# An encoder trunk's instruction order: the scheduler's other simulator

## The chip, the cores and the metric

The kernel runs on one core of one Trainium2 chip. The metric is device time in microseconds (us) of one execution of the whole program, as the median of several runs. One execution was also recorded by the hardware profiler; every row of a profile below comes from such a recorded execution.

## The reference

Two layers of an encoder over 512 positions of width 1024, in float32. Each layer normalises its input, projects it once, feeds three attention mixers that run side by side (A: grouped queries with normalised heads and a two-axis rotation; B: the difference of two softmaxes; C: latent attention with low-rank queries and keys), gates and merges them, projects and adds; then an MLP with a squared ReLU. A last normalisation follows.

```python
for l in range(DEPTH):                      # 2
    h = _rms_norm(x, ln1_g[l])
    proj = jnp.einsum('bsd,dn->bsn', h, w_in[l])
    (a_q, a_k, a_v, b_q, b_k, b_v, c_cq, c_ckv, c_kr, gate_logits) = _split_columns(proj)
    y_a = _gqa_axial(...)                   # 8 heads of 64 on 2 key heads
    y_b = _diff_attention(...)              # 8 heads, 2 x 32 for q and k, 64 for v
    y_c = _mla(...)                         # 8 heads, 64 + 32 for q and k, 64 for v
    y = jnp.stack([y_a, y_b, y_c], axis=2)
    gates = jax.nn.sigmoid(gate_logits.reshape(b, s, N_BRANCH, d))
    merged = jnp.sum(gates * jnp.einsum('bsne,ned->bsnd', y, w_branch[l]), axis=2)
    x = x + jnp.einsum('bsd,de->bse', merged, w_out[l])
    h2 = _rms_norm(x, ln2_g[l])
    ff = jnp.square(jax.nn.relu(jnp.einsum('bsd,df->bsf', h2, w_ff1[l])))
    x = x + jnp.einsum('bsf,fd->bsd', ff, w_ff2[l])
return _rms_norm(x, final_g)
```

## The kernel before

**Arithmetic.** Every float32 operand of a large product is split into a high part in TensorE's rounded float32 type and the rest (h and l in the names: wh, wl, fh, fl), and a product is three matmuls: high by high, high by rest, rest by high. A weight arrives by a DMA from SP's queue into a raw buffer wr (L53), ACT casts it to wh (L61), and GpSimd or VectorE subtracts to get wl (L67): GpSimd in pieces of 256 columns, VectorE in one piece. There are two raw buffers (NWR) and three of each part (NW). In the mixers all weights are split on GpSimd (PA = 5), in the MLP all on VectorE (PF = 0). The MLP's second product uses a scheme with seven block products in place of eight; its factors fa and fs come by DMA, some of them added on arrival by accumulating DMAs that GpSimd issues (L95, L96), and are split at L115 and L116.

**Stages.** The plan of a layer is a list of small items, each with a cost in us that serves only to arrange the list. First the projections of A and half of those of B (tm, L309 and L322). Then attention A, with the rest of B's projections woven in; attention B, with gates, branch products (gate, br, in L222) and C's low-rank products (c_rank); attention C, with the remaining gates, branches and C's per-head products (uq, uk). After that the last branches, the output projection (out, L222) and the MLP in three chunks, each a first product (ff, L222) and a second (ff, L1152).

**An attention unit.** One head and 128 queries: scores sc on TensorE (L222), the row maximum mx on VectorE (L585), the exponential p with its sum on ACT (L590), scaling by the reciprocal on VectorE (L595, for B L747), four transposes pT on TensorE (L601), the cast and the rest pt on ACT and VectorE (L604, L605), and for each pair of units the product with the values, pv (L222). Transposes of the projections (tp, L338) and the rotations (a_t, c_t, b_r) stand between. The pv, pT, tp and sc results lie in eight PSUM banks by tag: two for scores, two for transposes, one for values and statistics, three for projections and other long products.

**What sets the order.** The Python program issues its instructions in the order of the plan, with some steps deferred by a time of the plan (`defer`, for example transposes by LAG_T = 5.5 after their scores). That is not yet the order on the chip. At the end of the `TileContext` block a scheduler simulates the program and picks for each engine, whenever the simulated engine can take one, the earliest instruction of the program that is ready by then. The order so found is written into each engine's queue, SP's and GpSimd's DMA issues included, and the buffer that a tile gets among those of its tag is decided on the way. On the chip each queue then runs strictly in that order: an instruction whose operand is late holds up all behind it on its engine.

```python
    with tile.TileContext(nc) as tc:
        Trunk(tc, a, depth).go()
```

Of the kernel before, what the change touches and what calls it, by code (L numbers as in the profile page):

```python
# [1360 lines left out]
def build(nc, arrays, depth):  # L1361
    a = {k: nc.dram_tensor(k, v.shape, F32, kind="ExternalInput").ap() for k, v in arrays.items()}
    a["out"] = nc.dram_tensor("out", (128, 8, S), F32, kind="ExternalOutput").ap()
    with tile.TileContext(nc) as tc:
        Trunk(tc, a, depth).go()


# [8 lines left out]
```

## Time and profile before

| what | us |
|---|---|
| median of 3 runs | 1872.87 |
| lowest and highest | 1872.87, 1876.54 |
| the profiled execution's own time | 1872.25 |
| its span, first to last instruction | 1870.4 |
| TensorE busy in the span | 1820.2 |
| mean granted TensorE clock | 0.993 |

The span is what the profile's rows count from; their times are us from its start. A row of the stage table gives a stretch and, for each engine, busy time and number of instructions. A row of the waits gives who stood idle, for what, how long in total, how often, and the longest. In a timeline row the bracket at the end says how long the engine had been idle before it and what released it. PE is TensorE, PEld its weight loads, DVE VectorE, ACT ScalarE, POOL GpSimd, and SPq the queue in which SP issues DMAs. "br<-ya,wh" names the tile written and those read.

### The profile page before, as it was taken

The page shows a single profiled execution, that of the slowest core. Times are in us where ns is not written, and L with a number is a line of the kernel's source. Part 1 is how long each engine was busy: PE and PEld are TensorE (multiplying, and loading weights), DVE is VectorE, ACT ScalarE, POOL GpSimd, SP SyncE. Part 2 cuts the span into 40 slices and gives each one's busy share as a digit, 9 for nine tenths or more (in the row PEclk, how much of TensorE's full clock was granted, in tenths as well). Part 3 has the DMA queues.
Part 4 walks back from the last instruction along what each step waited for, and adds up shares of the span by engine and source line. Part 5 has one row for each costly group of instructions (what it writes and reads, how often), then busy time and mean ns, then how long its engine had stood idle before and what let it go on. Part 6 is the DMA issues. An engine that isn't in the chain of part 4 may idle for free.

```text
span 1870.4 us, 29990 instructions
## 1 busy us (share of the span) xinstructions
PE 1820.2 (97%) x10960; PEld 1603.4 (86%) x10960; DVE 1386.2 (74%) x2815; ACT 1011.1 (54%) x1852; POOL 461.6 (25%) x565
## 2 busy tenths in 40 slices
PE   8999999999999999999999999999999999999997
PEld 8998888777888898988999988878888888989897
DVE  8888889755665776867887888896566667777677
ACT  5577666655544434444446766665554444444443
POOL 4322443444101100101243224434440001011011
PEclk9999999999999999999999999999999999999998
DMA  5213331332153473745532134312232525637363
GB/s 164 79 41 85 102 108 43 96 84 81 51 170 101 100 188 92 172 121 147 138 105 68 40 91 124 92 46 84 82 91 68 163 90 125 163 94 187 100 147 94
DMA packets 85058, 197.25 MB, mean 105 GB/s; under 512 B 11952, under 2 KB 28720, under 8 KB 84912
## 3 DMA queue, kind: packets, MB, share of 16 engines
q1 hardware_dynamic: 74544, 178.56, 31.8%
q0 software_dynamic: 10368, 16.78, 6.0%
q8 instruction: 87, 1.43, 0.3%
q14 instruction: 59, 0.48, 0.1%
HBM read 174.32 MB, written 4.19 MB: 95 GB/s over the span
## 4 chain that ended last, share of the span: by engine, by line
PE 76%; DVE 12%; ACT 4%; DMA 4%; issue 2%; POOL 1%; SPq 0%; DVEq 0%; ACTq 0%; POOLq 0%
PE ff L222 18%; PE ff L1152 15%; PE gate L222 12%; PE br L222 6%; PE tm L309 5%; PE out L222 4%; PE sc L222 4%; PE pv L222 4%; PE pT L601 4%; PE c_rank L222 2%; DMA wr<-w 2%; DVE mx L585 1%; DMA fa<-wff 1%; DVE wl L67 1%; DVE p L747 1%
## 5 line engine op out<-in xcount | busy, mean ns | idle before, releaser
L67 POOL TENSOR_TENSOR wl<-wr,wh 128x256 fp32r<-128x256 f32 (+1 forms) x402 | 298.2, 772 | 534.9 <-ACT wh L61 503.1
L61 ACT CAST wh<-wr 128x1024 fp32r<-128x1024 f32 (+5 forms) x246 | 224.6, 914 | 343.2 <-PE ff L222 114.0
L1152 PE MATMUL ff<-h,fh 128*128 128x256 f32 x1792 | 324.1, 283 | 1.4 <-DVE x L1160 1.2
L222 PE MATMUL ff<-xg,wh 128*128 128x512 f32 x1024 | 315.6, 390 | 0.0
L1152 PEld LDWEIGHTS ff<-h,fh 128*128 128x128 f32 x1792 | 278.9, 192 | 3.1 <-issue 2.1
L1152 PE MATMUL ff<-h,fl 128*128 128x256 f32 x896 | 254.2, 285 | 1.5 <-DVE fl L116 1.3
L222 PE MATMUL gate<-xg,wh 128*128 128x512 f32 x768 | 241.5, 393 | 1.1 <-DVE c_K L230 1.1
L222 PEld LDWEIGHTS ff<-xg,wh 128*128 128x128 f32 x1024 | 191.7, 188 | 39.3
L115 ACT CAST fh<-fa 128x640 fp32r<-128x640 f32 (+1 forms) x144 | 108.8, 762 | 177.5 <-PE ff L1152 94.2
L309 PE MATMUL tm<-wh,xg 128*128 128x256 f32 x1024 | 202.4, 289 | 0.0
L585 DVE TENSOR_REDUCE mx<-sc 128x1 f32<-128x512 f32 x256 | 173.7, 683 | 36.7 <-PE sc L222 35.7
L222 PE MATMUL ff<-xg,wl 128*128 128x512 f32 x512 | 199.2, 389 | 0.0
L1152 PEld LDWEIGHTS ff<-h,fl 128*128 128x128 f32 x896 | 171.0, 192 | 4.7 <-DVE fl L116 4.1
L222 PEld LDWEIGHTS gate<-xg,wh 128*128 128x128 f32 x768 | 142.8, 188 | 29.9 <-PE pv L222 1.5
L309 PEld LDWEIGHTS tm<-wh,xg 128*128 128x128 f32 x1024 | 164.7, 192 | 0.2
L67 DVE TENSOR_TENSOR wl<-wr,wh 128x1024 fp32r<-128x1024 f32 (+3 forms) x117 | 134.0, 1145 | 25.2 <-ACT wh L61 25.2
L116 DVE TENSOR_TENSOR fl<-fa,fh 128x640 fp32r<-128x640 f32 (+1 forms) x144 | 124.6, 869 | 36.9 <-ACT fh L115 33.6
L222 PE MATMUL gate<-xg,wl 128*128 128x512 f32 x384 | 150.5, 392 | 0.0
L604 ACT CAST pt<-pT 128x512 fp32r<-128x512 f32 x192 | 112.0, 585 | 64.3 <-PE pT L601 62.1
L605 DVE TENSOR_TENSOR pt<-pT,pt 128x512 fp32r<-128x512 f32 x192 | 131.2, 685 | 19.3 <-ACT pt L604 17.7
L309 PE MATMUL tm<-wl,xg 128*128 128x256 f32 x512 | 145.0, 283 | 0.0
L601 PE MATMUL pT<-ident,p 128*128 128x128 f32 x768 | 116.2, 274 | 10.5 <-DVE p L595 4.8
(253 smaller groups left out, 3515.6 us busy)
## 6 DMA issues: line engine op xcount, KB each, us to landing
wr<-w SPq DMA_DIRECT2D x170, 512.0 KB, 3.6
fa<-wff SPq DMA_DIRECT2D x64, 320.0 KB, 3.4
wr<-w SPq DMA_DIRECT2D x52, 256.0 KB, 2.8
fa<-wff SPq DMA_DIRECT2D x32, 384.0 KB, 3.8
b_sq<-b_f SPq DMA_DIRECT2D x96, 64.0 KB, 2.8
b_sk<-b_f SPq DMA_DIRECT2D x96, 64.0 KB, 2.0
fa<-wff POOLq DMA_DIRECT2D x16, 320.0 KB, 4.8
fs<-wff SPq DMA_DIRECT2D x32, 160.0 KB, 2.8
```

Source lines behind the costliest of these rows:

```text
L61: t.nc.scalar.copy(wh, self.raw)
L67: e.tensor_tensor(wl[:, q], self.raw[:, q], wh[:, q].bitcast(F32), op=ALU.subtract)
L115: t.nc.scalar.copy(a, x)
L116: t.nc.vector.tensor_tensor(b, x, a.bitcast(F32), op=ALU.subtract)
L222: self.nc.tensor.matmul(out, l, r, start=(i == 0), stop=(i == n - 1))
L309: self.nc.tensor.matmul(ps, l, r, start=(u == 0 and i == 0 and tt % 2 == 0), stop=(u == 1 and tt % 2 == 1 and i == len(p) - 1))
L585: nc.vector.tensor_reduce(m, s, axis=AX.X, op=ALU.max, negate=True)
L601: nc.tensor.transpose(T[:, k], p[:, k * 128 : (k + 1) * 128], self.ident)
L604: nc.scalar.copy(h[:, :, q], T)
L605: nc.vector.tensor_tensor(lo[:, :, q], T, h[:, :, q].bitcast(F32), op=ALU.subtract)
L747: nc.vector.scalar_tensor_tensor(p0, p1, z1, p0, op0=ALU.mult, op1=ALU.add)
L1152: nc.tensor.matmul(bk[tag], x, y, start=(new and a == 0), stop=(part[1] == n and a == len(pairs) - 1), skip_group_check=True)
```

## The change

One argument is added. The scheduler's simulation is then the timeline simulator in place of the default one; both give times at which instructions start, finish and free buffers, from different models of the engines, queues and DMAs. The kernel's own program, its tiles, tags and buffer counts, and the order in which Python issues it are as before.

```diff
 def build(nc, arrays, depth):
     a = {k: nc.dram_tensor(k, v.shape, F32, kind="ExternalInput").ap() for k, v in arrays.items()}
     a["out"] = nc.dram_tensor("out", (128, 8, S), F32, kind="ExternalOutput").ap()
-    with tile.TileContext(nc) as tc:
+    with tile.TileContext(nc, schedule_with_timeline_sim=True) as tc:
         Trunk(tc, a, depth).go()
```

## The prediction, made before the changed kernel was run

> **What bounds the kernel now.** I read the page from the top, then busy time by stage, then the waits of TensorE, then single stalls in the timeline. The page first:
>
> ```profile
> span 1870.4 us, 29990 instructions
> PE 1820.2 (97%) x10960; PEld 1603.4 (86%) x10960; DVE 1386.2 (74%) x2815; ACT 1011.1 (54%) x1852; POOL 461.6 (25%) x565
> PEclk9999999999999999999999999999999999999998
> PE 76%; DVE 12%; ACT 4%; DMA 4%; issue 2%; POOL 1%; SPq 0%; DVEq 0%; ACTq 0%; POOLq 0%
> ```
>
> TensorE is busy for 97% of the span and holds 76% of the chain that ended last. The rest of that chain is where an order could matter. By stage (start; mixers of layer 0; output projection and MLP of layer 0, with the first part of layer 1; mixers of layer 1; its MLP; end), the columns being length, then busy us of PE, PEld, DVE, ACT, POOL, the granted clock, the DMA share and GB/s:
>
> ```profile
> 0.00:46.80 46.80, 39.37 (x295) 39.06 (x296) 37.49 (x82) 26.17 (x52) 22.15 (x27) 1.00 0.53 163
> 46.80:514.40 467.60, 453.69 (x2707) 391.10 (x2706) 360.31 (x806) 293.27 (x596) 166.97 (x215) 1.00 0.27 77
> 514.40:935.20 420.80, 419.88 (x2512) 375.23 (x2511) 300.33 (x512) 193.11 (x288) 47.14 (x48) 1.00 0.51 136
> 935.20:1449.60 514.40, 499.58 (x3018) 434.59 (x3017) 390.93 (x878) 311.42 (x635) 182.90 (x233) 0.99 0.28 81
> 1449.60:1823.60 374.00, 371.23 (x2141) 327.50 (x2140) 263.02 (x457) 168.55 (x251) 35.59 (x37) 1.00 0.50 134
> 1823.60:1870.40 46.80, 36.43 (x300) 35.90 (x298) 34.07 (x85) 18.59 (x30) 6.90 (x6) 0.88 0.37 94
> ```
>
> TensorE's idle time is 7.4, 13.9, 0.9, 14.8, 2.8 and 10.4 us, 50.2 in all. The two MLP stretches leave 3.7 us in 794.8: nothing to win there. Start and end are chains of dependent steps on single tiles. What an order can win lies in the two mixer stretches, 28.7 us.
>
> How tightly TensorE is packed while busy shows in the chain in order of time (start, length, what):
>
> ```profile
> 168.21 3.21 PE gate L222 x14
> 171.65 2.06 PE gate L222 x9
> 601.03 43.54 PE ff L222 x192
> 651.56 44.19 PE ff L1152 x364
> ```
>
> In the MLP 192 matmuls 512 wide run in one piece, 43.54 / 192 = 227 ns each, and 364 of 256 wide at 121 ns. In the mixers a gate's 24 matmuls are cut into pieces of 14 and 9 with attention work between: there the scheduler interleaves, in the MLP it keeps the order of the program. So **a different scheduling model can change much in the mixers and little in the MLP**.
>
> **The change, part by part.** It adds no instruction, removes none and changes no shape: the 29990 instructions and their durations stay. What moves is the order inside each of five queues (PE, DVE, ACT, POOL, SP, the last with its DMA issues; POOL's own accumulating DMAs too), and with it which buffer of a tag a tile gets. Every term is therefore a wait. The waits of TensorE (who, for whom: us, times, longest):
>
> ```profile
> PE tm L322 <- ACT wh L61: 6.6, 1, 6.6
> PE pT L601 <- DVE p L595: 4.8, 4, 2.4
> PE tp L338 <- DVE a_G L230: 4.0, 2, 2.1
> PE bc L222 <- DVE dg L377: 3.6, 1, 3.6
> PE pv L222 <- DVE pt L605: 2.0, 2, 1.0
> PE tp L338 <- DVE c_t L894: 1.8, 2, 0.9
> ...
> PE tp L338 <- DVE pt L605: 0.3, 2, 0.2
> ```
>
> The 22 rows of that answer, of which the first, the last and the largest stand here, add up to 41.9 us. The 6.6 (first weight) and the 3.6 (the last statistic) belong to start and end; **31.7 us** are waits that an order could in principle remove. Which of them did an order make? The longest place, in the timelines of ACT and PE:
>
> ```profile
> 450.51 0.20 ACT L590 ACTIVATION_READ_ACCUMULATOR p<-sc,mx,c_rq 128x1 f32 x1
> 454.76 1.05 ACT L61 CAST wh<-wr 128x1024 fp32r<-128x1024 f32 x1 [4.06 <-DMA wr<-w]
> 455.83 0.60 ACT L225 ACTIVATE c_Q<-uq 64x512 fp32r<-64x512 f32 x1
> 460.37 0.63 PE L601 MATMUL pT<-ident,p 128*128 128x128 f32 x4 [2.40 <-DVE p L595]
> ```
>
> ACT stands 4.06 us at the cast of a weight that has not landed. Behind it in ACT's queue are the evictions of c_Q and c_K and the next exponential; so DVE gets p late and TensorE waits 2.40 us. The cast was put ahead of work that was ready: the model that ordered it took the weight for landed. Layer 1 has its twin (4.8 us in the row for both). The second place, layer 0, DVE and PE:
>
> ```profile
> 65.78 1.22 DVE L67 TENSOR_TENSOR wl<-wr,wh 128x1024 fp32r<-128x1024 f32 x1
> 67.03 2.11 DVE L230 TENSOR_TENSOR a_G<-tp,a_G 64x512 fp32r<-64x512 f32 x3
> 68.56 0.63 PE L338 MATMUL tp<-ident,b_t 128*128 128x128 f32 x4 [2.12 <-DVE a_G L230]
> ```
>
> DVE splits a weight for 1.22 us ahead of the a_G that TensorE waits for (4.0 us over both layers). The third place, DVE and PE again:
>
> ```profile
> 324.45 2.33 DVE L889 TENSOR_TENSOR c_t<-c_t,rope 128x1024 f32<-128x1024 f32 x1
> 327.14 0.68 DVE L605 TENSOR_TENSOR pt<-pT,pt 128x512 fp32r<-128x512 f32 x1
> 327.87 0.97 PE L222 MATMUL pv<-pt,b_V 128*128 128x256 f32 x6 [1.02 <-DVE pt L605]
> ```
>
> A long rotary step stands ahead of the pt that TensorE waits for, and its last step ahead of c_t: 2.0 + 1.8 = 3.8 us over both layers. These three make 4.8 + 4.0 + 3.8 = **12.6 us**.
>
> A stall costs a second time, through the clock. Two neighbouring stretches at the third place, then the three others like the second of them:
>
> ```profile
> 326.60:330.00 3.40, 1.78 (x13) 1.33 (x11) 3.40 (x7) 0.86 (x2) 2.47 (x2) 1.00 0.01 5
> 330.00:333.50 3.50, 3.20 (x13) 3.04 (x14) 2.44 (x9) 1.49 (x5) 0.26 (x1) 0.51 0.17 42
> 988.80:992.20 3.40, 3.40 (x18) 3.40 (x18) 1.81 (x3) 1.86 (x3) 0.16 (x1) 0.50 0.01 2
> 1251.60:1255.10 3.50, 3.40 (x13) 3.19 (x14) 2.43 (x8) 1.69 (x6) 0.46 (x1) 0.51 0.11 35
> 1381.30:1384.80 3.50, 3.50 (x11) 2.92 (x12) 3.12 (x5) 2.71 (x5) 0.17 (x1) 0.51 0.25 98
> ```
>
> TensorE was busy 1.78 of 3.40 us, and for the 3.5 us after that the granted clock was 0.51. Four such stretches stand in the mixers, each costing about 3.4 x 0.5 = 1.7 us, **6.8 us** together, and each follows one of the three places. The Trainium skill, page "TensorE: Matmul & The Clock Gate", section "Why this matters for your kernels", asks only for no idle gap over about 3 us; by that limit no stall here (2.40 us the longest row above) would cost clock, and removing them would bring 12.6 us and no more. The rows decide against that limit: the clock fell after gaps well under it.
>
> So what the order visibly made is 12.6 + 6.8 = **19.4 us**; that is the gain if a better-informed order removes all three places and makes no new one. All of 31.7 + 6.8 = 38.5 us is the outer bound of a gain. From the other side, no row bounds what a worse order would add; the nearest is the price of one bad placement, 2.40 us and at worst 1.7 us of clock. I take half of 19.4, 9.7 us: the faults are of a kind that a closer time line would see (a weight not yet landed, an engine still occupied), but every order over in-order queues makes faults of its own where the chip differs from its model. Everything else I cost at nothing, covered by TensorE's own work: the casts and splits of the MLP and the loads behind them lie beside 790 us of packed matmuls. If that cover went, the next in line would be DVE, 300.33 of 420.8 us there, so not soon.
>
> The sum: profiled execution 1872.25 us (span 1870.4 and 1.85 around it) minus 9.7 = 1862.6. The median of the runs, 1872.87, lies 0.6 above the profiled one; so **1863 us**.
>
> **The rivals.**
>
> *Slower: the single weight queue.* Weights have two raw buffers, and all their loads leave through SP's queue, with the small copies of the heads. SP's and ACT's waits:
>
> ```profile
> SPq L53 <- POOL wl L67: 301.5, 117, 10.0
> ACT wh L61 <- DMA wr<-w: 33.8, 15, 4.3
> wr<-w SPq DMA_DIRECT2D x170, 512.0 KB, 3.6
> ```
>
> 117 loads wait at the head of SP's queue for POOL to finish a split, so a load seldom has slack; in 15 cases ACT already stands at a cast for its weight. If the new order puts a copy whose source is late ahead of a load, or a cast ahead of an exponential more often, each such fault is a copy of the first place: 2.40 us and, for half of them, 1.7 of clock, 3.25 on average. It decides from 19.4 / 3.25 = 6 new faults on, the whole visible gain. At one in ten of those 117 loads (12 faults) it adds 39.0, less the 19.4: +19.6, **1892 us**. For it: the two buffers, and that SP's order is shuffled whenever the model's times shift. Against it: TensorE lost only 31.7 us in waits under an order that made the same kind of error, and 2.4 us was its longest.
>
> *No difference.* The new order may be almost the old one, or the switch may have no effect on it at all; or the waits come from two transpose banks and two raw buffers, and only move. Then 1872.9 us, within 3.7. For it: the MLP, two fifths of the span, follows the program, and nine of TensorE's 22 rows are below 1 us. Against it: in the mixers the cuts (14 and 9) depend on modelled times, and all those change.
>
> **How the numbers follow.** A measurement of this kernel can tell about 0.2%, 3.7 us, from no change. Faster by more, as forecast: 0.45, with its own range from 1847 (two thirds of the outer 38.5) to 1869. Slower by more, the queue: 0.38. Within 0.2%: 0.17, of which 0.03 that nothing changes at all. The range for 8 in 10 must hold most of both signs, and reaches from 1847 to 1900, the latter 14 faults instead of 12 and a little more; I leave out about 0.1 on either side.
>
> **What would show it.** Right: the count of instructions and TensorE's 10960 matmuls unchanged; the MLP stretches as long as before; the mixer stretches some 5 us shorter each; the rows for p, a_G, pt and c_t smaller; fewer than four half-clock stretches; ACT's 33.8 us at unlanded weights reduced. Wrong towards slower: that 33.8 or TensorE's waits grown, gaps of 2 to 4 us at pT or sc, more stretches at half clock, DVE idle inside the mixers. Wrong towards nothing: the same cuts at the same places. What would upset the whole argument is a loss in the MLP stretches, where I expect no change of order that matters.

## The result and the profile after

The changed kernel takes 1904.11 us (median of 4 runs, 1901.67 to 1908.42), beside 1873.28 of the kernel before (4 runs): a ratio of 1.0166, 95% interval 1.0154 to 1.0178. It is slower by 31 us, and the time lies above the range. The profiled execution took 1901.67 us. Its page:

```profile
span 1899.9 us, 29929 instructions
PE 1829.5 (96%) x10960; PEld 1617.8 (85%) x10960; DVE 1377.4 (72%) x2815; ACT 1004.8 (53%) x1852; POOL 463.1 (24%) x565
PEclk9999998999999999999999999989999999999998
```

The counts of TensorE, VectorE, ScalarE and GpSimd are those of before, so nothing was added or taken away in their work. The row of the clock has two 8s inside the span, where before had nines. To see where the time went, both traces are cut at the same instructions: the first and last scores of attention A, B and C, and the middle of B's scores. The stretches of before (start:end, length, then busy us of PE, PEld, DVE, ACT, POOL with counts, granted clock, DMA share, GB/s): A of layer 0 up to B, the two halves of B, C, and the halves of B in layer 1:

```profile
76.08:171.26 95.18, 94.40 (x733) 89.01 (x731) 83.19 (x206) 70.47 (x147) 24.89 (x34) 1.00 0.18 55
171.26:244.13 72.87, 71.34 (x375) 58.77 (x374) 63.10 (x126) 47.17 (x102) 25.23 (x32) 1.00 0.40 111
244.13:326.33 82.20, 80.07 (x454) 66.94 (x453) 70.68 (x170) 54.02 (x118) 31.96 (x39) 1.00 0.25 70
339.92:508.72 168.80, 163.76 (x844) 135.63 (x843) 105.19 (x226) 98.29 (x184) 70.02 (x92) 1.00 0.28 78
...
1092.76:1165.54 72.78, 71.24 (x375) 58.78 (x374) 62.99 (x126) 47.17 (x102) 25.15 (x32) 1.00 0.42 112
1165.54:1247.73 82.19, 80.06 (x455) 66.92 (x453) 70.67 (x170) 54.02 (x118) 31.98 (x39) 1.00 0.23 69
```

The same stretches of the changed kernel:

```profile
77.52:180.05 102.53, 100.51 (x759) 94.73 (x758) 84.80 (x207) 69.83 (x149) 26.94 (x36) 1.00 0.18 52
180.05:266.60 86.55, 82.80 (x419) 67.94 (x418) 66.15 (x131) 52.38 (x108) 35.44 (x45) 1.00 0.41 114
266.60:350.14 83.54, 72.04 (x380) 60.76 (x379) 66.57 (x169) 49.29 (x110) 20.59 (x24) 0.86 0.16 43
363.10:525.13 162.03, 159.40 (x826) 134.29 (x825) 101.44 (x221) 94.23 (x179) 70.32 (x92) 1.00 0.28 81
...
1114.23:1193.66 79.43, 72.38 (x369) 58.99 (x367) 59.85 (x118) 46.90 (x100) 30.52 (x39) 1.00 0.42 116
1193.66:1282.21 88.55, 80.45 (x428) 67.29 (x429) 71.40 (x182) 53.65 (x119) 22.40 (x29) 0.90 0.17 47
```

Length after less length before, over both layers:

| stretch | us |
|---|---|
| start of a layer to the first score of A | -4.3 |
| A, up to the first score of B | +14.7 |
| B, both halves | +28.0 |
| last score of B to first of C | +2.0 |
| C | -13.5 |
| last branches, output projection, MLP, up to the last product | +1.5 |

**A is longer because it does more.** It holds 759 matmuls in place of 733 and is busy for 6.1 of the added 7.35 us in layer 0: products that before ran later are pulled forward. **B is longer although it does less**: 419 + 380 matmuls in place of 375 + 454 in layer 0. Its second half is the place: TensorE is idle for 11.5 of 83.54 us (before 2.1 of 82.20), and the granted clock is 0.86. **C is shorter** by 6.8 us in each layer. In layer 0 4.4 us of that is busy time, with 18 matmuls fewer, and 2.4 us is idle time. The waits of TensorE in the changed kernel (who, for whom: us, times, longest):

```profile
PE sc L222 <- ACT p L590: 14.3, 18, 1.8
PE bT L776 <- DVE bR L769: 8.1, 4, 2.5
PE tm L322 <- ACT wh L61: 6.7, 1, 6.7
PE bc L222 <- DVE dg L377: 4.7, 1, 4.7
PE pT L601 <- DVE pt L605: 4.4, 4, 2.1
PE pT L601 <- DVE p L595: 3.4, 4, 1.1
PE tm L322 <- DVE wl L67: 3.3, 2, 1.7
...
PE pv L222 <- DVE pt L605: 2.2, 5, 0.6
...
PE tp L338 <- DVE c_t L894: 1.3, 2, 1.0
...
PE tp L338 <- DVE a_G L230: 0.2, 1, 0.2
```

The old large rows shrank: p 4.8 to 3.4, a_G 4.0 to 0.2, c_t 1.8 to 1.3. Two new ones stand on top, scores waiting for the exponential that frees their bank (before 3.7 us) and B's transposes bT waiting for the scaled result bR (before 0.4). All rows together are 63.3 us, before 41.9. Both new rows belong to attention's own chains. One such place, layer 0, TensorE in the timeline:

```profile
299.32 0.51 PE L222 MATMUL sc<-b_sk,b_sq 96*128 96x512 f32 x1 [0.22 <-ACT p L590]
301.17 0.79 PE L222 MATMUL sc<-b_sk,b_sq 96*128 96x512 f32 x1 [1.34 <-ACT p L590]
304.04 1.09 PE L776 MATMUL bT<-ident,bR 128*128 128x128 f32 x4 [2.07 <-DVE bR L769]
304.92 1.06 PE L601 MATMUL pT<-ident,p 128*128 128x128 f32 x4
...
310.33 1.22 PE L222 MATMUL gate<-xg,wh 128*128 128x512 f32 x2
```

From 293.90, where the last low-rank product of C ends, to 310.33 TensorE has nothing but scores, transposes, statistics and products with the values, which hang on results of VectorE and ScalarE. No gate lies between them to fill the gaps. Before, at the same place of B, the low-rank products ran on to the next gate:

```profile
300.15 0.39 PE L222 MATMUL c_rank<-xg,wl 128*128 128x512 f32 x1
302.23 0.70 PE L222 MATMUL gate<-xg,wh 128*128 128x512 f32 x2
```

The gaps cost a second time. Stretches of the changed kernel about that place, and one of layer 1:

```profile
296.50:299.90 3.40, 2.35 (x11) 1.38 (x10) 3.40 (x12) 1.82 (x6) 0.62 (x1) 0.99 0.44 124
299.90:313.60 13.70, 10.36 (x35) 8.40 (x36) 11.71 (x36) 7.41 (x17) 0.00 (x0) 0.51 0.20 49
323.80:327.20 3.40, 3.33 (x14) 3.17 (x15) 3.40 (x7) 3.20 (x8) 0.91 (x1) 0.51 0.00 0
337.40:344.20 6.80, 4.01 (x15) 3.44 (x16) 6.53 (x25) 3.24 (x9) 0.00 (x0) 0.50 0.00 0
1265.90:1276.10 10.20, 5.89 (x21) 4.37 (x20) 9.48 (x37) 4.72 (x13) 0.00 (x0) 0.50 0.02 7
```

In the trace's record of the clock, nine stretches between the start and the end run at half clock, 51.1 us long in all (before four, 13.6 us). TensorE is busy in them for 40.4 us (before 13.2). If half of that busy time is what the clock costs, it costs 20.2 us after and 6.6 before: by this estimate 13.6 us more. The page gives a smaller growth: of the 29.5 us by which the span grew, TensorE's busy time has 9.3 and its idle time 20.2, of which 10.3 lie inside the stretches at half clock. How much of that idle time the slower clock brought about, by making the chains through TensorE longer, no run separates.

### The profile page after: what moved, and what is told of

Read it like the earlier page. It is cut to its first block, busy times and chain, and to the rows that moved or that the text cites. A ratio compares the mean times of both kernels' runs of the same rounds, so it can differ in the third digit from the quotient of the medians.

```text
span 1899.9 us, 29929 instructions
## 1 busy us (share of the span) xinstructions
PE 1829.5 (96%) x10960; PEld 1617.8 (85%) x10960; DVE 1377.4 (72%) x2815; ACT 1004.8 (53%) x1852; POOL 463.1 (24%) x565
## 4 chain that ended last, share of the span: by engine, by line
PE 71%; DVE 4%; DMA 3%; ACT 2%; issue 0%; SPq 0%; POOL 0%; DVEq 0%; ACTq 0%; POOLq 0%
PE ff L222 18%; PE ff L1152 13%; PE gate L222 11%; PE br L222 6%; PE tm L309 5%; PE out L222 5%; PE sc L222 4%; PE pv L222 3%; DMA fa<-wff 3%; PE pT L601 2%; PE c_rank L222 1%; DVE fl L116 1%; PE tm L322 1%; DVE mx L585 1%; PE uq L222 1%
## 5 line engine op out<-in xcount | busy, mean ns | idle before, releaser
L222 PE MATMUL ff<-xg,wh 128*128 128x512 f32 x1024 | 315.4, 389 | 0.0
L222 PE MATMUL gate<-xg,wh 128*128 128x512 f32 x768 | 245.9, 396 | 0.2 <-DVE c_K L230 0.2
L222 PEld LDWEIGHTS ff<-xg,wh 128*128 128x128 f32 x1024 | 191.8, 188 | 39.4
L222 PE MATMUL ff<-xg,wl 128*128 128x512 f32 x512 | 199.4, 389 | 0.0
L309 PE MATMUL tm<-wh,xg 128*128 128x256 f32 x1024 | 196.4, 285 | 0.0
L222 PEld LDWEIGHTS gate<-xg,wh 128*128 128x128 f32 x768 | 143.8, 190 | 29.1 <-ACT c_sq L808 0.4
L309 PEld LDWEIGHTS tm<-wh,xg 128*128 128x128 f32 x1024 | 162.9, 191 | 3.0
L605 DVE TENSOR_TENSOR pt<-pT,pt 128x512 fp32r<-128x512 f32 x192 | 131.2, 684 | 44.3 <-ACT pt L604 43.7
L222 PE MATMUL gate<-xg,wl 128*128 128x512 f32 x384 | 152.2, 396 | 0.0
L309 PE MATMUL tm<-wl,xg 128*128 128x256 f32 x512 | 145.3, 284 | 0.0
L590 ACT ACTIVATE p<-sc,mx 128x512 f32<-128x512 f32 x128 | 88.1, 690 | 78.8 <-DVE mx L585 61.0
```

Of the source, the lines that this page charges most:

```text
L222: self.nc.tensor.matmul(out, l, r, start=(i == 0), stop=(i == n - 1))
L309: self.nc.tensor.matmul(ps, l, r, start=(u == 0 and i == 0 and tt % 2 == 0), stop=(u == 1 and tt % 2 == 1 and i == len(p) - 1))
L590: nc.scalar.activation(p, s, AF.Exp, bias=m, scale=1.0 if scale is None else scale, accum_out=z)
L605: nc.vector.tensor_tensor(lo[:, :, q], T, h[:, :, q].bitcast(F32), op=ALU.subtract)
```

## The experiments

The expectations number the theories. 1: products of C's low-rank stage hold the three long PSUM banks, because the buffers that their evictions write are handed out in the order of the program, behind results of B. 2: TensorE's order, which spends the independent products early. 3: too few of those buffers (tag s4). 4: the order of ScalarE and VectorE. The later ones are stated where they come up. "Lost" in them is a stretch's length less the time that its matmuls take at the median start-to-start distance of their kind in the trace of before. Ratios are to the kernel before on the same chip, with the 95% interval.

**e1. More buffers.** A scratch area for DMAs is made smaller to make room.

```diff
-        self.NS4, self.NWR, self.NW, self.NTMP, self.NP = 25, 2, 3, 4, 4
+        self.NS4, self.NWR, self.NW, self.NTMP, self.NP = 27, 2, 3, 4, 4
-    nc = bacc.Bacc("TRN2", target_bir_lowering=False, num_devices=1)
+    nc = bacc.Bacc("TRN2", target_bir_lowering=False, num_devices=1, dynamic_dma_scratch_size=8192)
```

> The changed kernel with 27 buffers of the tag s4 in place of 25 (paid for by 8 KB less scratch for the software DMA descriptors). Theory 1 (the three long-product PSUM banks stay full because the buffers for the evicted c_rank results are handed out in program order, behind an attention result that is late): the first attention results still come first in that order, so 1904 us within 5. Theory 2 (TensorE spends its independent products early, and the second half of attention B has none left, banks or not): 1904 within 5 too. Theory 3 (there are simply too few buffers of the tag): 1880 to 1890, and the c_rank evictions in the second half of attention B come within 3 us of the last matmul.

Measured: 1910.46 us, 1.0191 (1.0172 to 1.0210). Two more buffers bring nothing, even allowing for what e4 finds the setting to cost; theory 3 falls.

**e2. The low-rank results get their buffers early.** As e1, and five buffers are claimed by one-column writes ahead of the low-rank products.

```diff
+            st["cf"] = [self.s4("c_f") for _ in range(3)]
+            st["cs"] = [self.s4("c_sq", dtype=F32) for _ in range(2)]
+            for y in st["cf"]:
+                nc.gpsimd.memset(y[:, 0, 0:1].bitcast(F32), 0.0)
...
-                    x = self.s4("c_f")
+                    x = st["cf"][j]
```

> The changed kernel with 27 buffers of s4, and the five tiles for C's low-rank q results claimed by one-column memsets ahead of the products, so that their eviction waits for no attention result. TensorE still may run its c_rank products ahead. Theory 1: the evictions follow within 3 us, attention B loses 20 to 30 us less in both layers together, and the whole takes 1875 to 1885 us. Theory 2: the products are spent early all the same, 1895 to 1905. Theory 3 doesn't tell this from the run with 27 buffers.

Measured: 1898.28 us, 1.0124 (1.0102 to 1.0147). The next gate now starts at 292.65 us in place of 310.33, so the banks do come free. The second half of B, stretches as above:

```profile
265.35:344.48 79.13, 71.23 (x374) 60.47 (x372) 65.08 (x166) 46.97 (x107) 19.48 (x25) 0.87 0.16 46
```

TensorE is still idle for 7.9 us and the clock is 0.87. Against e1 it is 12.2 us faster, so the banks are a part; most of the loss has another cause. The time lies where theory 2 expected it.

**e3. Low-rank products in the order of the program.**

```diff
-            self.nc.tensor.matmul(out, l, r, start=(i == 0), stop=(i == n - 1))
+            m = self.nc.tensor.matmul(out, l, r, start=(i == 0), stop=(i == n - 1))
+            if pin and i == 0:
+                self.tc.keep_in_program_order(m)
...
-                self.mm(ps, self.fm_pairs(w, 0, self.xg))
+                self.mm(ps, self.fm_pairs(w, 0, self.xg), pin=True)
```

> The changed kernel, 25 buffers, with the first matmul of each of the five c_rank products pinned behind the TensorE instruction traced before it, so these products cannot run ahead of attention. Theory 1: no bank stays full, 1875 to 1887 us. Theory 2: the products last longer into the second half of attention B, a part of the loss returns, 1885 to 1897. Theory 3: 1900 to 1908, since the buffers are as few as before.

Measured: 1901.01 us, 1.0139 (1.0122 to 1.0156). Pinning this one kind moves little, and neither theory 1's time nor theory 2's is reached.

**e4. The kernel before with the buffers of e1.**

> The kernel before, default scheduler, with the same 27 buffers: the control of the two runs with 27. All theories: 1868 to 1876 us, since its evictions of c_rank already follow within some us of the products; if it gains over 10 us, buffers are short under both schedulers and theory 3 gains weight.

Measured: 1878.32 us, 1.0023 (1.0012 to 1.0035). The setting of e1 and e2 costs 3 to 4 us by itself; it is no help to the old order either.

For the next runs the order of a queue is taken from the other kernel and imposed on the scheduler as bare order, without waits. `ORDER` holds, for each engine that is to be held, the numbers of its instructions; the numbers are the same in both kernels, as they are given when Python issues them.

```diff
+def keep(tc):
+    have = {i.name: i for i in tc.nc.cur_bb.bb.instructions}
+    for queue in json.loads(zlib.decompress(base64.b85decode(ORDER))).values():
+        names = [f"I-{n}" for n in queue if f"I-{n}" in have]
+        for p, q in zip(names, names[1:]):
+            tc.add_manual_dep(have[q], p, mybir.DependencyInfo(mybir.DependencyClass.NoSync, mybir.DependencyReason.DATA),
+                              reason="order")
...
         Trunk(tc, a, depth).go()
+        keep(tc)
```

**e5. The change, with TensorE's whole queue as before.** (ORDER: TensorE's queue of before.)

> The changed kernel with TensorE's queue held to the order of the kernel before; the timeline simulator still orders ACT, DVE, POOL and SP. Theory 2 (TensorE's order carries the loss: independent products are spent early and attention falls behind): 1868 to 1882 us, and 74 to 78 us of TensorE work again in the second half of attention B. Theory 4 (the loss lies in the order of ACT and DVE, which serve attention late): 1890 to 1905.

Measured: 1898.30 us, 1.0131 (1.0105 to 1.0156). The halves of B are repaired, and a loss turns up in A (layer 0: first half of B, second half, A):

```profile
183.81:257.70 73.89, 71.27 (x376) 58.90 (x375) 62.22 (x129) 48.16 (x106) 25.02 (x33) 1.00 0.41 109
257.70:340.42 82.72, 78.85 (x455) 67.44 (x453) 73.18 (x168) 52.94 (x115) 30.90 (x39) 1.00 0.25 70
...
84.04:183.81 99.77, 94.54 (x732) 88.97 (x732) 83.56 (x205) 70.08 (x146) 24.75 (x34) 1.00 0.18 53
```

A has before's 732 matmuls and takes 4.6 us more than before, the start of layer 0 takes 8.0 us more, and C loses its gain. The expected time was missed: TensorE's old order meets the new order of the others there. In the start TensorE waits 4.3 us for a_kr and 3.8 for two splits (before 0.8 and none), in A 4.8 us for z (before none), all of them results of VectorE.

**e6. The kernel before, with TensorE's whole queue as after the change.** (Default simulator, ORDER: TensorE's queue of after.)

> The converse: the default simulator, with TensorE's queue held to the order of the changed kernel. Theory 2: 1895 to 1912 us, with some 60 to 70 us of TensorE work and 18 us or more lost in the second half of attention B. Theory 4: 1873 to 1885.

Measured: 1964.11 us, 1.0472 (1.0457 to 1.0488). Some 64 of the 91 us are lost in B, with 43.7 us of scores waiting for exponentials. It is three times the loss of the change and beyond both expectations: TensorE's new order is far worse beside the default simulator's order of the others than beside its own.

**e7. The change, with ScalarE and VectorE as before.** (ORDER: their two queues of before.)

> The changed kernel with the queues of ACT and DVE held to the order of the kernel before; TensorE, POOL and SP as the timeline simulator orders them under that. Theory 4: 1868 to 1882 us. Theory 2: TensorE's own order is chosen anew from when ACT and DVE finish, so a part comes back, 1885 to 1905.

Measured: 1995.54 us, 1.0644 (1.0628 to 1.0660). That is beyond both expectations. With ScalarE and VectorE as before, the simulator's TensorE loses far more, in A, B and C alike, so putting their two orders back is no cure. As TensorE's order is chosen anew beside them, the run does not tell whose order carries the loss of the change.

**e8. All independent products in the order of the program.** As e3, for the gates, the branches and the half-width projections (L309) too; the first of these edits:

```diff
-            self.mm(ps, self.fm_pairs(wg, 0, self.xg))
+            self.mm(ps, self.fm_pairs(wg, 0, self.xg), pin=True)
```

> The changed kernel with the first matmul of every gate, branch, c_rank and half-width projection product pinned behind the TensorE instruction traced before it, so that none of them runs ahead of attention work that the program puts first. Theory 2: 1875 to 1890 us, the first half of attention B holding 66 to 70 us of TensorE work instead of 79. Theory 4: 1895 to 1908. If pinning holds TensorE up behind late attention work, 1900 or more with stalls at the pinned matmuls.

Measured: 1960.92 us, 1.0465 (1.0447 to 1.0482). Only the last of the three expectations has such a time, and its stalls at the pinned products did not come: the largest wait is again that of scores for exponentials, 36.0 us. The order in which Python issues the products is not the order that worked before, which a simulation had rearranged; pinning to the program is a third order, and worse.

The orders of the queues plainly belong together. So the next four runs hold all five queues at once, and choose the stage.

**e9. The change, with all five queues as before.**

> Timeline simulator as in the change, but all five queues (TensorE, VectorE, ScalarE, GpSimd, SP) held to the order of the kernel before. Theory 5, the switch acts through the order of the queues alone, and the orders belong together: the time of before, 1870 to 1880 us, no stretch at half clock more than before's four in the mixers. Rival, theory 6, the switch acts through something else as well (which buffer of a tag a tile gets, or the waits that the schedule writes into the program): 1885 us or more.

Measured: 1873.20 us, 0.9993 (0.9982 to 1.0003). The switch acts through the order of the queues alone, and theory 6 falls.

**e10. All five queues as before, in attention B only.** (ORDER: the numbers from 2338 to 4409 and from 12464 to 14535, B's scores and what is issued among them.)

> Timeline simulator, with all five queues held to before's order only for the instructions that the program issues in attention B (scores of B, the gates, branches and low-rank products issued among them), in both layers; start, attention A, attention C and MLP keep the new order. Theory 5 with the loss in attention B alone: TensorE's time without work in B falls from 31.5 and 29.3 us to about 10.5 per layer, so about 40 us off 1902: 1858 to 1870 us, faster than before. If new stalls arise where the two orders meet, as when one queue alone was held: 1885 to 1910. If the loss is set up in attention A already, whose order stays new (products pulled forward by 6.9 us): 1880 to 1900 with B still starved at its end.

Measured: 1875.86 us, 0.9998 (0.9988 to 1.0008). Putting back the order of B alone takes away 28 of the 31 us, and the halves of B are 72.8 and 82.2 us long again in both layers. The time did not fall below that of before, which was expected: A, up to B, is still 4.3 and 5.7 us longer than in before, which eats what C and the start of layer 1 gain.

**e11. The kernel before, with attention C as after the change.** (Default simulator; ORDER: after's five queues, numbers 4410 to 6446 and 14536 to 16572.)

> The kernel before with its default simulator, all five queues held to the order of the changed kernel only for the instructions issued in attention C, in both layers. Theory 5 with the gain in C a gain of order: attention C loses 6.3 to 7.2 us per layer in place of 11.0 to 11.8, so 8 to 10 us less: 1862 to 1867 us. If attention C is shorter after the change only because products were spent earlier: 1871 to 1877. If the seams cost: 1880 or more.

Measured: 1866.46 us, 0.9956 (0.9942 to 0.9970). The new order of C is a real gain of 8 us, not only work moved.

**e12. The change, with all five queues as before in A and B.** (ORDER: numbers below 4410 and from 11108 to 14535.) C, the MLP and the start of layer 1 keep the new order.

> Timeline simulator, all five queues held to before's order for what is issued up to the end of attention B in layer 0, and from attention A to the end of B in layer 1; attention C, the MLP and the start of layer 1 keep the new order. Theory 5: before, less the gains of the new order in C (4.7 and 4.6 us) and at the start of layer 1 (5.6), that is 1854 to 1862 us, faster than both kernels. If the gains are only work moved from one stage to another: 1870 to 1877. If the seams cost: 1880 or more.

Measured: 1863.11 us, 0.9936 (0.9922 to 0.9950), 11 us below before and faster than both kernels. Attention C in both layers:

```profile
344.22:505.69 161.47, 159.23 (x826) 134.39 (x825) 101.61 (x222) 93.31 (x178) 66.73 (x87) 1.00 0.28 80
1258.89:1420.37 161.48, 159.22 (x826) 134.39 (x825) 101.75 (x222) 93.34 (x178) 66.53 (x87) 1.00 0.27 80
```

168.80 us have become 161.47, and the start of layer 1 is 5.6 us shorter. About 3 us in each layer go back at the seam from B to C.

**e13. TensorE's queue alone as before, in attention B only.** (ORDER: TensorE's numbers of e10.)

> Timeline simulator; only TensorE's queue is held to before's order, and only for what is issued in attention B; the other four queues and all other stages are the simulator's own. Theory 7, the loss in B is carried by TensorE's order there: the halves of B take 73 to 75 and 82 to 84 us as when all five queues were held, and the time is that of that run, 1870 to 1882 us. Rival, theory 8, the orders belong together inside B too: a loss of 15 us or more remains in B, 1890 us or more.

Measured: 1876.18 us, 1.0016 (1.0004 to 1.0027). The halves of B in both layers:

```profile
177.54:251.14 73.60, 71.00 (x375) 58.94 (x374) 62.03 (x128) 47.99 (x105) 24.45 (x32) 1.00 0.38 102
251.14:334.00 82.86, 78.99 (x454) 67.35 (x452) 73.30 (x169) 52.92 (x115) 31.07 (x39) 1.00 0.26 69
1101.47:1175.18 73.71, 71.11 (x376) 59.04 (x374) 62.07 (x128) 48.09 (x105) 24.44 (x32) 1.00 0.38 101
1175.18:1259.02 83.84, 80.59 (x454) 68.95 (x452) 72.92 (x169) 52.79 (x115) 31.62 (x39) 0.98 0.24 67
```

They sum to 314.0 us, where before has 310.0 and the change 338.1, and the time is that of e10. So theory 8 falls: holding TensorE's order in B is enough. It does not follow that the other orders have no part, for the simulator arranges them around TensorE's. In B of layer 0, with instructions matched by line and tiles, VectorE's stand on average 1.3 places and ScalarE's 0.6 from where they stand in before, but 5.1 and 5.8 from where the change has them.

**e14. The other four queues as before, in attention B only.** (ORDER: VectorE's, ScalarE's, GpSimd's and SP's numbers of e10.)

> Timeline simulator; VectorE, ScalarE, GpSimd and SP are held to before's order for what is issued in attention B, TensorE's queue and all other stages are the simulator's own. Theory 7: the second half of B stays starved, 1895 us or more, and at least as bad as the change itself if the queues now fit each other less. Rival, the other engines' order carries the loss: 1870 to 1882 us.

Measured: 1959.48 us, 1.0462 (1.0449 to 1.0476), as theory 7 expected. The other four queues, put back without TensorE's, do not help; TensorE's own order, chosen anew beside them, fits them less. The second half of B in layer 0 shows it:

```profile
277.44:375.41 97.97, 82.80 (x410) 68.13 (x409) 71.10 (x169) 51.20 (x113) 28.61 (x35) 0.86 0.20 53
```

**e15. Only the spread of the products as before, in attention B.** (ORDER: of TensorE's numbers of e10 those that write sc, gate, br, tm and c_rank.)

> Timeline simulator; on TensorE in attention B only the sequence of the scores and the independent products (gate, br, tm, c_rank) is held to before's, so that the products are spread over the scores as before, while transposes and the products with the values go where the simulator puts them. If the spread of the products is what counts: 1870 to 1885 us, hardly a stretch at half clock in B. If the finer order counts as well: 1890 us or more.

Measured: 1888.80 us, 1.0084 (1.0072 to 1.0096). It takes away about half of the loss, between the two expectations. The halves of B in layer 0 and one of the waits of TensorE (the lines of this kernel are numbered 3 higher, L225 for L222):

```profile
179.28:253.88 74.60, 69.97 (x359) 57.20 (x359) 59.62 (x125) 46.78 (x102) 23.35 (x32) 1.00 0.36 93
253.88:338.50 84.62, 81.01 (x460) 69.93 (x459) 72.03 (x175) 53.79 (x118) 30.77 (x38) 0.98 0.27 74
```

```profile
PE sc L225 <- ACT p L593: 13.1, 16, 1.9
```

The halves of B sum to 317.5 us over both layers, beside 314.0 in e13 and 338.1 in the change: inside B the spread of the products is most of the matter. VectorE's order there lies between the two kernels (4.3 places from before, 3.4 from the change), so most of B's loss goes without VectorE's old order. The seams on both sides of B take 5.4 us more in sum than in e13, nearly all of it from B to C, and the waits of scores for exponentials are almost those of the change (14.3 us).

## Why the prediction was wrong

**What bounds the kernel: right.** TensorE is busy for 96% of the span. The output projection and the MLP are as long as before in sum (+2.0 us in layer 0, -3.0 in layer 1), as predicted from their packed order.

**Nothing but order changes: right, and shown by e9.** One item on the list was wrong: the count of all instructions fell from 29990 to 29929, while the engines' work stayed at 10960, 2815, 1852 and 565.

**The three places that the old order had made: half right.** The waits for p, a_G, pt at pv and c_t were 4.8 + 4.0 + 2.0 + 1.8 = 12.6 us and are 3.4 + 0.2 + 2.2 + 1.3 = 7.1. The gains lie where such places stood: 5.6 us at the start of layer 1, which includes one half-clock stretch of before, and the shorter C. The new order of C alone is worth 8 us (e11); with the MLP and the start of layer 1 it is 11 us (e12). That fits the mechanism, though no run removes the three places alone. That e12 measures 1863.11, the time that was forecast for the change, is luck: it keeps only a part of the new order, and the forecast was made by halving the gain of the three places.

**The step that failed** is the one after it: "From the other side, no row bounds what a worse order would add; the nearest is the price of one bad placement, 2.40 us and at worst 1.7 us of clock. I take half of 19.4". A bad order was priced as single bad placements. What the change did was to spread the fillers badly. In B the attention chains leave TensorE gaps, which the fillers fill, that is the gates, branches and low-rank products; the new order has spent too many of them by the middle of B, in layer 0 visibly in A and the first half, and in the second half the gaps stand open, as in the 16 us from 293.90 on. This term measures +28 us (e10 takes it away whole, e13 all but 4 us), where the prediction had nothing. In layer 1 the first half of B does no more work than before and is 6.7 us longer, so fillers spent early are not the whole of it there; e13 shows only that holding TensorE's order takes the loss away in that half too (73.7 us).

**The clock: right in kind, wrong in extent.** The reading that gaps well under 3 us cost clock held: the 13.7 us at half clock that begin at 299.90 follow a stretch in which TensorE was busy for 2.35 of 3.40 us, and no single wait of the mixers in the changed kernel is longer than 2.55 us. The prediction counted the clock as a gain of up to 6.8, half of it in the sum; it became a loss, of 13.6 by the estimate above. The Trainium skill, page "TensorE: Matmul & The Clock Gate", section "A second HAM failure mode: psum-queue depth-cycling", describes the like in another kernel, a clock that swings because TensorE idles briefly and often between groups of matmuls. The trace is in line with it: ahead of eight of the nine stretches TensorE was busy for 1.3 to 2.4 of 3.40 us.

**The rival "slower" had the right side and the wrong mechanism.** Its 1892 us came from late weights; that it lies nearer to 1904 than the forecast is luck. ScalarE's wait at unlanded weights is almost unchanged:

```profile
ACT wh L61 <- DMA wr<-w: 35.4, 22, 6.0
```

That is 35.4 us against 33.8, and of it 4.2 us lie in B's halves (before 1.8). In the same halves ScalarE waits 60.8 us for row maxima ahead of the exponential (before 35.5). TensorE's waits that name a weight are small (6.7 us for the first one, as before, and 3.3 for two splits), and the loss in B goes in e13, where SP's and GpSimd's queues are the simulator's own. SP's wait for GpSimd's splits did grow, from 301.5 to 325.9 us, without reaching TensorE in these rows. Of the signs listed towards slower, more waits of TensorE, gaps of about 2 us at sc and pT and more half clock all came; the growth of the 33.8 did not. The range ended at 1900 because it was built from 14 copies of that fault.

**What stays open.** Why the timeline simulator spends B's fillers early is not shown; no run bears on its own times. In e13 VectorE's and ScalarE's orders came back close to before's together with TensorE's, and no run holds TensorE's old order beside the change's order of those two in B alone. e15, which leaves VectorE's order farther from before's, takes away 20.6 of the 28 us in B's halves, but only half of the whole loss. Of theory 1, e2 shows about 12 us of effect under the settings of e1, which cost 3 to 4 us by themselves in e4; whether the two effects add up is open. The half-clock stretches were read from the records, and no run removes them alone.

## What to carry to other kernels

Where independent products fill the gaps of a latency-bound chain, the thing to look at in a schedule is how evenly they last: compare matmuls and idle time of the busiest engine per half of each stage, before looking at single waits. An order is one thing across all queues: with one or two queues held to another schedule throughout, the kernel was 23 to 121 us slower than before (e5, e6, e7); holding all of them, stage by stage, let two schedules be combined into one faster than either (e12). One queue was enough only in one stage, and with a simulator that fitted the others to it (e13). Where two schedulers can be had, compare them stage by stage and take from each the stage in which it is better.

## What the runs showed of the hardware

In both kernels every half-clock stretch between the start and the end is about a multiple of 3.4 us long (3.4, 6.8, 10.2 or 13.7). In the changed kernel eight of the nine follow 3.40 us with 1.3 to 2.4 us of TensorE work, but busy time alone doesn't tell when one comes. The 10.20 us at half clock from 1265.90 in the changed kernel follow a stretch in which TensorE was busy all the time:

```profile
1262.50:1265.90 3.40, 3.40 (x28) 3.14 (x27) 3.05 (x8) 1.24 (x3) 1.59 (x2) 0.98 0.18 47
```

Of its matmuls sixteen write only two columns or one:

```profile
1263.41 0.95 PE L222 MATMUL bss<-blk,bsq 128*128 128x2 f32 x8
1264.21 1.03 PE L364 MATMUL c_ss<-ones,c_sq 128*128 128x1 f32 x8
```

They count as busy in the records. That such narrow products keep the clock up less than wide ones is what these rows suggest; no run tested it.
